# Two weight tiles on ScalarE's DMA queue, products of zeros at the start, and a last residual sum without GpSimd

## The chip, the cores and the metric

The kernel runs on one core of a Trainium2 chip. The metric is the device time of one execution in microseconds (us). A core has a matrix engine (TensorE, "PE" in the rows; its weight loads are "PEld"), VectorE ("DVE"), ScalarE ("ACT"), GpSimd ("POOL") and SyncE ("SP"). SP computes nothing here: it issues the transfers, which 16 DMA engines then carry out. Each engine takes its own instructions strictly in program order and waits on semaphores for the others.

## The reference

Two transformer blocks run one after the other on 256 tokens of width 1024, batch 1, in float32. The first block has two layers; each is

```
h = rmsnorm(x); proj = h @ w_in            # attention, indexer, HGRN and gate columns
x = x + (sigmoid(ga)*(attn @ w_proj_attn) + sigmoid(gb)*(hgrn @ w_proj_hgrn)) @ w_out
x = x + (silu(g) * u) @ w_ffn_out          # g, u = rmsnorm(x) @ w_ffn_in
```

The second block has one layer with a mixer of forgetting attention and a causal convolution, and a feed-forward network. Its last step is what the kernel ends with:

```
y = swiglu_ffn(h, w_ffn_in, w_ffn_out)
x = x + g2 * rms_norm(y, ffn_post_g)       # the result, 256 x 1024
```

## The kernel before

**Tiling.** Every weight matrix is cut into tiles of 128 x 1024 floats (512 KB), stored in the order of use in one array `W`. A tile is loaded into one of 4 `raw` buffers. ScalarE rounds it to `wH` and VectorE computes the rest `wL = raw - wH` (`do_split`); there are 6 buffers of each. TensorE multiplies with both in a reduced format and adds three products, wH·xH + wH·xL + wL·xH (`mm3`). A tile serves 24 products of 128 x 256 in the first layers. The input x, transposed, is the constant `xT`; it arrives in four pieces of 256 KB (`load_x(0)` to `load_x(3)`), each holding two of the eight chunks of the inner dimension. For every chunk ScalarE writes `xH` and VectorE `xL` (`scaled_split`), with a scale that comes from the array `params`. The first two weight tiles are loaded in halves (`CUT = 2`): the first half holds chunks 0 to 3, the second 4 to 7.

**Order.** The program is first recorded as a list of operations with their dependencies (`Recorder.record`). `Recorder.issue` then plays that list with estimated costs, picks on each engine the available operation of the highest urgency (the estimated length of the chain behind it plus `bias`), and emits the instructions of all engines in the order of the starts that it found. The plan has an engine "DMA" for the queue of SP, whose loads cost their bytes at 360 GB/s plus a latency, and starts at `FIRST_LOAD`. The chip then runs that fixed order, with its own durations. Table sets of ScalarE are loaded where the plan needs a function outside the current set (`load_tables`).

**The start.** SP issues params, the four pieces of x, the first half of weight tile 0, a piece of the constants, the second half of tile 0, a small weight matrix (`b<-in_small`), positions, and tiles 1 to 3. TensorE's first instruction is the first product of tile 0.

**The end.** `post(n, acc, last)` takes the four accumulators of the last product (token half t, column half h), and for each t computes 1/rms on VectorE from two squares that ScalarE sums (`inv_rms`, with the chain of short [128,1] operations in `rsqrt`), multiplies the accumulators with the weight row (`u`), and adds u·r to the residual in `xt` (an `E` buffer). For t = 1 the last step is one fused VectorE instruction for each h. In the last call t = 0 is done otherwise: ScalarE scales u by r and GpSimd adds it to `xt`. Each quarter is then sent out by a DMA of SP.

In the rows every recorded operation has line L408, the line that emits it, so they are told apart by tile names: `c` is any constant (xT, params, the matrix of ones), `t` any temporary of 512 columns, `side` and `mm` are accumulators, `small` the short columns.

Of the kernel before, what the change touches and what calls it, by code (L numbers as in the profile page):

```python
# [19 lines left out]
AF = mybir.ActivationFunctionType  # L20
# [3 lines left out]
D, T, NCH = 1024, 256, 8  # L24
GROUPS = 4
ON_V = (0, 4)
LAST = 0.0
FF, NJ = 2816, 11
LINE = 128

# [2 lines left out]
PLACE, ROOM = 28, 64  # L33

SCRATCH = 8192
OUT_SHAPE = [256, 1024]
EPS = 1e-6
NEG = -1e30
# [275 lines left out]
SETS = ("exp_and_others", "natural_log_exp_and_others", "silu_and_others")  # L314
TABLES = {AF.Exp: {0, 1}, AF.Tanh: {0, 2}, AF.Ln: {1}, AF.Silu: {2}, AF.Sin: {2}}
FIRST_LOAD = 500.0
LOAD_LATENCY, GATE_BIAS, LATER = 2000.0, 30000.0, -1e6
PRM_BIAS = 5000.0
TABLE_BIAS = -2000.0
# [32 lines left out]
class Recorder:  # L352
    def __init__(self, nc):
        self.ops = []
        self.bias, self.feed = 0.0, None
        self.load_tables = nc.scalar.preload_act_table_set
        for name, real in (("PE", nc.tensor), ("V", nc.vector), ("S", nc.scalar), ("DMA", nc.sync), ("G", nc.gpsimd)):
            setattr(self, name, Engine(self, name, real))

    def record(self, engine, real, method, args, kw):  # L360
# [50 lines left out]
    @staticmethod  # L411
    def cost(engine, method, args, kw, views, outs):
        n = int(np.prod((outs or views)[0].shape[1:]))
        psum = any(v.buf.space == "PSUM" for v in views)
        if engine == "DMA":
            v = (outs or views)[0]
            return max(v.shape[0] * n * 4 / 360.0, 640.0)
        if engine == "PE":
            if method == "transpose":
                return 109.0  # L420
            m = int(np.prod(args[1].shape[1:]))
            if args[1].dtype == F32R:
                return max(n * 0.4265, 109.0)
            cost = max(n, m) * 1.667 + 3.0
            if args[1].shape[0] == 64:

                return cost / 2

            return (cost + 81.0) / 4 if m == 32 else (cost + 53.0) / 2 if m == 64 and n > 64 else cost
        if engine == "S":  # L430
            ptr = sum(isinstance(kw.get(k), View) for k in ("bias", "scale"))
            return (51 if psum else 94) + 0.833 * n + 93 * ptr + (93 if "accum_out" in kw else 0)
        if method in ("max",):
            n = int(np.prod(args[1].shape[1:]))
        fast = not psum and method in ("tensor_copy", "tensor_scalar")
        ptr = sum(isinstance(a, View) for a in args[2:{"tensor_scalar": 4, "scalar_tensor_tensor": 3}.get(method, 2)])
        return (68 if method != "memset" else 7) + n / (1.92 if fast else 0.96) + 61 * ptr

    def issue(self):
# [12 lines left out]
                ops[d].users.append((op, lat))  # L452
        for op in reversed(ops):
            tail = max([u.rank + lat for u, lat in op.users], default=0.0)
            op.rank = tail + op.cost + (LOAD_LATENCY if op.engine == "DMA" else 0.0)
            op.urgency = op.rank + op.bias
            if QUANT and op.engine == "PE":
                op.urgency = op.urgency // QUANT * QUANT

        names = ["PE", "V", "S", "DMA", "G"]  # L460
        free_at = dict.fromkeys(names, 0.0)
        free_at["DMA"] = FIRST_LOAD
        pending = {e: [] for e in names}
        avail = {e: [] for e in names}
        slots, waiting, first, line = {}, {}, {}, {}
# [23 lines left out]
        while len(order) < len(ops):  # L489
# [91 lines left out]
                busy, left = busy + inside * rate, cost - inside  # L581
            op.start, op.end = t, t + cost
            free_at[e] = op.end
            done = op.end + (LOAD_LATENCY if e == "DMA" else 0.0)
            order.append(op)
            for b in op.bufs:
                if b.space == "PSUM":
# [43 lines left out]
def program(tc, I, out, pw, cw, tap=None, stop=None):  # L631
# [11 lines left out]
    with es:  # L643
# [8 lines left out]
        def body():  # L652
# [13 lines left out]
            def bank(tag="mm"):  # L666
                return new(psum, [128, 512], F32, tag=tag, bufs=4)
# [29 lines left out]
            A = lambda o, i, f, **k: S.activation(o, i, f, **k)  # L697


            prm = new(const, [128, I["params"].shape[1]])  # L700
            R.bias = PRM_BIAS
            DMA.dma_start(prm, I["params"])
# [23 lines left out]
            def load(i):  # L726
                if i < NT and i not in raw:
                    raw[i] = new(wp, [128, 1024], F32, tag="raw", bufs=N_RAW)
                    for k, c in enumerate(cuts(i)):
                        R.bias = FIRST[k] if i == 0 else 0.0  # L730
                        DMA.dma_start(raw[i][:, c], I["W"][i][:, c])
                    R.bias = 0.0

            def do_split(i):
# [797 lines left out]
            def post(n, acc, last):  # L1532
                gp = G[n][3]
                for t in range(2):
                    R.bias = (LAST if last else EARLY) if t == int(last) else 0.0
                    r = inv_rms(lambda h: acc[2 * t + h])
                    for h in range(2):
                        s = slice(h * 512, h * 512 + 512)
                        u = t512()
                        tt(u, acc[2 * t + h], gp[:, s], OP.mult)  # L1540
                        if last and t == 0:
                            A(u, u, AF.Copy, scale=r)
                            R.G.tensor_tensor(xt[:, t, s], xt[:, t, s], u, OP.add)
                        else:
                            stt(xt[:, t, s], u, r, xt[:, t, s], OP.mult, OP.add)
                        if last:
                            DMA.dma_start(out[t * 128:t * 128 + 128, s], xt[:, t, s])
                R.bias = 0.0
# [193 lines left out]
```

## Time and profile before

| | |
|---|---|
| time, three runs | 1110.72 us median (1109.97 to 1111.0) |
| the profiled execution | 1110.12 us, of which the span on the page is 1108.0 us |
| TensorE matmul busy | 1073.6 us, 97% of the span |
| VectorE busy | 855.5 us, 77% |
| ScalarE busy | 589.8 us, 53% |
| GpSimd busy | 7.4 us, 1% |
| moved by DMA | 217.47 MB, mean 196 GB/s |

TensorE is busy nearly all the time. What it is not busy adds up to 34.4 us (1108.0 - 1073.6), and most of that lies at the two ends: the first 9.57 us and the last 9 us. A change at the ends is therefore read from the time lines of the first 20 us and the last 10 us, and a share of busy time over the whole span says nothing about it.

### The profile page before, as it was taken

To read this page: it belongs to the slowest core of one execution; us is meant where nothing else is said; L and a number is where in the kernel's file an instruction comes from. 1 tells how busy PE (TensorE), PEld (TensorE's weight loads), DVE (VectorE), ACT (ScalarE), POOL (GpSimd) and SP (SyncE) were. 2 spreads that over 40 slices of the span, in tenths; PEclk is the share of its full clock that TensorE was granted. 3 is DMA by queue.
4 is the path that set the end of the run, shared out by engine and by line. 5 is a ranking of instruction groups with operands and counts; after the bars stand their busy time and mean duration, and the time that the engine had idled before them with its cause. 6 is when DMAs were issued, how large, how long until landed. Compare 5 with 4: busy or idle time off the path is not lost.

```text
span 1108.0 us, 22974 instructions
## 1 busy us (share of the span) xinstructions
PE 1073.6 (97%) x9388; PEld 1010.8 (91%) x9388; DVE 855.5 (77%) x1590; ACT 589.8 (53%) x902; POOL 7.4 (1%) x16
## 2 busy tenths in 40 slices
PE   6999999999999999999999999999899979999996
PEld 6988999999999999889999999999798568999995
DVE  7999968798966589999778999756799677454554
ACT  5745585544544467446846444444645665444442
POOL 1000000000000000000000000000000000000000
PEclk9999999999999999999999999999999999999999
DMA  7544536689966543645366889666377126556550
GB/s 262 177 156 156 166 125 191 221 302 335 348 221 212 196 149 131 210 135 172 118 197 223 293 329 370 212 196 197 116 217 199 63 77 200 178 184 218 189 173 38
DMA packets 59992, 217.47 MB, mean 196 GB/s; under 512 B 6872, under 2 KB 10096, under 8 KB 56816
## 3 DMA queue, kind: packets, MB, share of 16 engines
q1 hardware_dynamic: 59888, 216.02, 58.5%
q8 instruction: 73, 1.20, 0.4%
q14 instruction: 31, 0.25, 0.1%
HBM read 214.19 MB, written 1.63 MB: 195 GB/s over the span
## 4 chain that ended last, share of the span: by engine, by line
PE 85%; DVE 7%; ACT 3%; DMA 3%; issue 1%; SPq 0%; DVEq 0%; ACTq 0%
PE mm L408 59%; PE side L408 26%; DMA raw<-in_W 3%; DVE wL L408 3%; ACT t L408 1%; DVE t L408 1%; ACT wH L408 1%; DVE small L408 1%; DVE sc L408 1%; DVE c L408 1%; DVE b L408 1%; DVE xL L408 0%; ACT b L408 0%; ACT L615 0%; ACT c L408 0%
## 5 line engine op out<-in xcount | busy, mean ns | idle before, releaser
L408 ACT ACTIVATE wH<-raw 128x1024 fp32r<-128x1024 f32 (+1 forms) x390 | 369.3, 970 | 385.3 <-PE mm L408 217.1
L408 DVE TENSOR_TENSOR wL<-raw,wH 128x1024 fp32r<-128x1024 f32 (+1 forms) x390 | 424.6, 1111 | 137.1 <-ACT wH L408 136.0
L408 PE MATMUL mm<-xH,wH 128*128 128x256 f32 x1760 | 485.8, 279 | 9.6 <-ACT wH L408 9.6
L408 PE MATMUL mm<-xL,wH 128*128 128x256 f32 x1760 | 486.8, 278 | 0.5 <-DVE xL L408 0.5
L408 PE MATMUL mm<-xH,wL 128*128 128x256 f32 x1760 | 485.0, 278 | 0.8 <-DVE wL L408 0.8
L408 PEld LDWEIGHTS mm<-xH,wH 128*128 128x128 f32 x1760 | 330.0, 188 | 13.6 <-ACT wH L408 9.6
L408 PEld LDWEIGHTS mm<-xL,wH 128*128 128x128 f32 x1760 | 330.8, 188 | 4.9 <-issue 2.8
L408 PEld LDWEIGHTS mm<-xH,wL 128*128 128x128 f32 x1760 | 330.4, 188 | 3.1 <-DVE wL L408 1.7
L408 PE MATMUL side<-t,wH 128*128 128x256 f32 x704 | 122.5, 275 | 0.0
L408 PEld LDWEIGHTS side<-t,wH 128*128 128x128 f32 x704 | 106.5, 188 | 0.0
L408 PE MATMUL side<-t,wL 128*128 128x256 f32 x352 | 96.8, 275 | 0.0
L408 ACT ACTIVATE t<-t 128x512 f32<-128x512 f32 (+2 forms) x80 | 48.9, 619 | 41.3 <-DVE t L408 40.6
L408 PEld LDWEIGHTS side<-t,wL 128*128 128x128 f32 x352 | 66.1, 188 | 0.0
L408 DVE SCALAR_TENSOR_TENSOR E<-E,b 128x1024 f32<-128x1024 f32 x48 | 58.0, 1220 | 7.4 <-DMA E<-in_ada 7.4
L408 PE MATMUL side<-wH,t 128*128 128x512 f32 x176 | 56.6, 391 | 0.0
L408 DVE TENSOR_TENSOR t<-t,t 128x512 f32<-128x512 f32 (+2 forms) x78 | 53.1, 680 | 3.8 <-ACT t L408 2.9
L408 PE MATMUL mm<-b,wH 128*128 128x256 f32 x256 | 44.3, 275 | 0.0
L408 PE MATMUL side<-E,wH 128*128 128x256 f32 x256 | 44.1, 276 | 0.0
L408 PE MATMUL mm<-wH,xH 128*128 128x512 f32 x96 | 38.7, 410 | 3.1 <-ACT xH L408 2.7
L408 DVE TENSOR_TENSOR t<-mm,rstd 128x512 f32<-128x512 f32 (+1 forms) x50 | 33.7, 677 | 10.1 <-PE mm L408 9.7
L408 PE MATMUL mm<-wL,xH 128*128 128x512 f32 x96 | 39.1, 407 | 1.0 <-DVE wL L408 1.0
L408 PE MATMUL mm<-wH,xL 128*128 128x512 f32 x96 | 39.1, 409 | 0.0
(205 smaller groups left out, 1161.8 us busy)
## 6 DMA issues: line engine op xcount, KB each, us to landing
raw<-in_W SPq DMA_DIRECT2D x348, 512.0 KB, 4.4
E<-in_ada SPq DMA_DIRECT2D x24, 1024.0 KB, 7.3
b<-c SPq DMA_DIRECT2D x16, 128.0 KB, 5.6
c<-in_xT SPq DMA_DIRECT2D x4, 256.0 KB, 4.7
raw<-in_W SPq DMA_DIRECT2D x4, 256.0 KB, 5.4
b<-in_c SPq DMA_DIRECT2D x2, 512.0 KB
out_y<-E SPq DMA_DIRECT2D x4, 256.0 KB, 2.0
c<-E SPq DMA_DIRECT2D x4, 143.0 KB, 5.6
```

The costliest lines, as they stand in the source:

```text
L408: op.emit = lambda: getattr(real, method)(*[get(a) for a in args], **{k: get(a) for k, a in kw.items()})
```

## The change

There are three edits. The loads of weight tiles 0 and 1 (four halves) are issued by ScalarE and not by SP; for the plan this is a further engine "Q" beside "DMA". VectorE clears a tile of 128 x 128 floats, and TensorE multiplies it with itself 18 times, with a bias that puts these products ahead of all others. And in the last `post`, the half t = 0 ends like t = 1, with the fused VectorE instruction; the bias of the two halves changes with it.

```diff
-LAST = 0.0
+WARM = 18
+LOADERS = "DMA", "Q"
+ON_Q = 2
...
-        for name, real in (("PE", nc.tensor), ("V", nc.vector), ("S", nc.scalar), ("DMA", nc.sync), ("G", nc.gpsimd)):
+        for name, real in (("PE", nc.tensor), ("V", nc.vector), ("S", nc.scalar), ("DMA", nc.sync), ("Q", nc.scalar), ("G", nc.gpsimd)):
...
-        names = ["PE", "V", "S", "DMA", "G"]
+        names = ["PE", "V", "S", "DMA", "Q", "G"]
         free_at = dict.fromkeys(names, 0.0)
-        free_at["DMA"] = FIRST_LOAD
+        free_at["DMA"] = free_at["Q"] = FIRST_LOAD
...
+            zero = new(const, [128, 128])
+            V.memset(zero, 0.0)
+            warm = bank("side")
+            R.bias = 1e6
+            for _ in range(WARM):
+                PE.matmul(warm[:, :128], zero, zero, start=True, stop=True, skip_group_check=True)
+            R.bias = 0.0
...
-                        DMA.dma_start(raw[i][:, c], I["W"][i][:, c])
+                        (R.Q if i < ON_Q else DMA).dma_start(raw[i][:, c], I["W"][i][:, c])
...
             def post(n, acc, last):
...
-                    R.bias = (LAST if last else EARLY) if t == int(last) else 0.0
+                    R.bias = EARLY if t == 0 else 0.0
...
-                        if last and t == 0:
-                            A(u, u, AF.Copy, scale=r)
-                            R.G.tensor_tensor(xt[:, t, s], xt[:, t, s], u, OP.add)
-                        else:
-                            stt(xt[:, t, s], u, r, xt[:, t, s], OP.mult, OP.add)
+                        stt(xt[:, t, s], u, r, xt[:, t, s], OP.mult, OP.add)
```

Since the plan is made anew, instructions move beyond these lines. With buffer numbers left out, the order of the changed kernel differs from the old one in the first 1490 of some 8700 rows of TensorE, in the first 392 of some 1500 of VectorE, and in the first 191 of some 830 of ScalarE; then it is the same until the last `post`.

SP at the start. `c_87` (before) and `c_94` (now) are x, `in_params` the scales, `raw_106`/`raw_129` tiles 0 and 1 before. Before:

```order
L408 DMA c_83<-in_params 128x331
L408 DMA c_87<-in_xT 128x512 x4
L408 DMA raw_106<-in_W 128x512
L408 DMA c_108<-in_consts 128x194
L408 DMA raw_106<-in_W 128x512
L408 DMA b_81_118<-in_small 128x544
L408 DMA t_42_124<-in_pos 128x256
L408 DMA raw_129<-in_W 128x512
```

Now (`raw_105`, `raw_128` and `raw_152` are tiles 2, 3 and 4):

```order
L412 DMA c_85<-in_params 128x331
L412 DMA c_94<-in_xT 128x512 x2
L412 DMA raw_105<-in_W 128x1024
L412 DMA raw_128<-in_W 128x1024
L412 DMA c_94<-in_xT 128x512 x2
L412 DMA raw_152<-in_W 128x1024
L412 DMA c_172<-in_consts 128x194
L412 DMA b_83_177<-in_small 128x544
```

The halves of tiles 0 and 1 are gone from SP. The tiles 2 and 3 of 512 KB each now stand ahead of the last two pieces of x, and the small matrix stands behind tile 4.

ScalarE at the start, before:

```order
L615 ACT_TABLE_LOAD
L408 ACTIVATE c_100<-c_100 128x4
L408 ACTIVATE xH_110<-c_87,c_83 128x256 x5
L408 ACTIVATE wH_126<-raw_106 128x512
L408 ACTIVATE xH_110<-c_87,c_83 128x256 x2
L408 ACTIVATE wH_126<-raw_106 128x512
```

Now (`raw_87` is tile 0, `raw_101` tile 1, `t_29` to `t_32` are squares of x):

```order
L412 DMA raw_87<-in_W 128x512 x2
L412 DMA raw_101<-in_W 128x512 x2
L412 ACT_TABLE_LOAD
L412 ACTIVATE wH_112<-raw_87 128x512
L619 ACT_TABLE_LOAD
L412 ACTIVATE c_118<-c_118 128x4
L412 ACTIVATE wH_112<-raw_87 128x512
L412 ACTIVATE xH_140<-c_94,c_85 128x256 x4
L412 ACTIVATE t_29_158<-c_94 128x512
L412 ACTIVATE t_30_165<-c_94 128x512
L412 ACTIVATE xH_140<-c_94,c_85 128x256 x4
L412 ACTIVATE t_31_189<-c_94 128x512
```

Four issues lead, the rounding of tile 0 stands ahead of x, and there is a second table load in the stretch. The last two squares (`t_31`, `t_32`) and all of x stand ahead of the rounding of tile 1.

VectorE at the end, from the product with the weight row for the accumulator t = 1, h = 1 (`t_2120` before, `t_2122` now) back to 1/rms of t = 1. Before:

```order
L408 TENSOR_TENSOR t_2120_13579<-side_12059,b_1865_11740 128x512
L408 TENSOR_SCALAR small_13581<-small_13576 128x1
L408 SCALAR_TENSOR_TENSOR small_13585<-small_13576,small_13581 128x1
L408 TENSOR_TENSOR small_13587<-small_13585,small_13581 128x1
L408 SCALAR_TENSOR_TENSOR small_13589<-small_13587 128x1
```

Now:

```order
L412 SCALAR_TENSOR_TENSOR E_10347<-t_2111_13557,small_13577,E_10347 128x512
L412 TENSOR_SCALAR small_13600<-small_13597 128x1
L412 SCALAR_TENSOR_TENSOR E_10347<-t_2112_13569,small_13577,E_10347 128x512
L412 SCALAR_TENSOR_TENSOR small_13604<-small_13597,small_13600 128x1
L412 TENSOR_TENSOR t_2122_13606<-side_12080,b_1867_11761 128x512
L412 TENSOR_TENSOR small_13609<-small_13604,small_13600 128x1
L412 SCALAR_TENSOR_TENSOR small_13611<-small_13609 128x1
```

The two sums of t = 0 (`E_10347`) now stand between the first short operations of t = 1; the rows after them are the same in both.

## Rows read from the trace of the kernel before

**Rows 1.** The page: busy time of TensorE and VectorE, share of the span, instructions.

```profile
PE 1073.6 (97%) x9388; PEld 1010.8 (91%) x9388; DVE 855.5 (77%) x1590; ACT 589.8 (53%) x902; POOL 7.4 (1%) x16
```

**Rows 2.** Stretches: length, busy (instructions) by engine, granted clock, DMA share, GB/s.

```profile
2.00:16.00 14.00, 5.98 (x31) 5.57 (x32) 8.89 (x21) 9.64 (x20) 2.15 (x4) 1.00 0.96 323
16.00:39.00 23.00, 22.73 (x196) 22.32 (x195) 22.15 (x50) 16.47 (x22) 0.23 (x1) 1.00 0.56 186
160.00:1098.00 938.00, 924.78 (x7860) 876.18 (x7859) 708.12 (x1216) 488.97 (x728) 0.53 (x1) 0.99 0.60 200
```

**Rows 3.** Time line, start: start us, us, instruction, count [idle before <-releaser].

```profile
0.73 1.28 ACT L615 ACT_TABLE_LOAD   x1 [0.73 <-PEq L1734]
1.18 1.84 SPq L408 DMA_DIRECT2D c<-in_xT  x4
4.78 0.91 ACT L408 ACTIVATE xH<-c,c 128x256 fp32r<-128x256 f32 x2 [1.04 <-DMA c<-in_xT]
8.89 0.63 ACT L408 ACTIVATE wH<-raw 128x512 fp32r<-128x512 f32 x1 [0.78 <-DMA raw<-in_W]
9.57 0.58 PE L408 MATMUL mm<-xH,wH 128*128 128x256 f32 x1 [9.57 <-ACT wH L408]
12.19 1.14 ACT L408 ACTIVATE t<-c 128x512 f32<-128x512 f32 x2
```

**Rows 4.** Time line of TensorE, 13.2 to 16.5 us and 154 us.

```profile
13.24 0.41 PE L408 MATMUL mm<-xH,wH 128*128 128x256 f32 x1
13.45 0.39 PE L408 MATMUL mm<-xL,wH 128*128 128x256 f32 x1
16.42 0.38 PE L408 MATMUL mm<-xH,wL 128*128 128x256 f32 x1
154.37 0.38 PE L408 MATMUL side<-b,b 128*128 128x128 f32 x2
154.58 0.39 PE L408 MATMUL side<-b,AT 128*128 128x128 f32 x2
```

**Rows 5.** Time line of VectorE, 11.5 to 20.4 us.

```profile
11.56 0.29 DVE L408 CAST t<-t 128x256 f32<-128x256 int32 x1
12.93 1.48 DVE L408 TENSOR_TENSOR t<-t,t 128x512 f32<-128x512 f32 x2
14.44 0.42 DVE L408 TENSOR_TENSOR t<-t 128x256 f32<-128x256 f32 x1
14.78 0.72 DVE L408 TENSOR_TENSOR b<-b,b 128x544 fp32r<-128x544 f32 x1
15.68 4.70 DVE L408 TENSOR_TENSOR wL<-raw,wH 128x512 fp32r<-128x512 f32 x5
```

**Rows 6.** The time line of TensorE, those that waited between 39 and 90 us.

```profile
70.62 0.50 PE L408 MATMUL mm<-wL,xH 128*128 128x512 f32 x1 [0.84 <-DVE wL L408]
85.99 0.47 PE L408 MATMUL mm<-wH,xH 128*128 128x512 f32 x1 [0.41 <-DVE t L408]
```

**Rows 7.** A later wait of TensorE, and the stretch around it (columns of rows 2).

```profile
793.68 0.29 PE L408 MATMUL mm<-xH,b 128*8 128x256 f32 x1 [2.53 <-ACT xH L408]
790.00:800.00 10.00, 6.52 (x40) 4.47 (x39) 8.14 (x19) 6.91 (x14) 0.00 (x0) 0.83 0.27 100
```

**Rows 8.** Time line of VectorE and GpSimd, last 9 us.

```profile
1100.38 2.48 POOL L408 TENSOR_TENSOR E<-E,t 128x512 f32<-128x512 f32 x2 [894.55 <-DVE small L408]
1100.41 1.25 DVE L408 SCALAR_TENSOR_TENSOR small<-small,small 128x1 f32<-128x1 f32 x1
1101.69 1.19 DVE L408 TENSOR_TENSOR small<-small,small 128x1 f32<-128x1 f32 x1
1102.91 0.16 DVE L408 SCALAR_TENSOR_TENSOR small<-small 128x1 f32<-128x1 f32 x1
1103.37 0.16 DVE L408 TENSOR_TENSOR small<-small,small 128x1 f32<-128x1 f32 x1
1103.76 1.42 DVE L408 SCALAR_TENSOR_TENSOR E<-t,small,E 128x512 f32<-128x512 f32 x2
```

More of the change, by code (lines that the diff above doesn't have):

```diff
@@ L414, in cost @@
         psum = any(v.buf.space == "PSUM" for v in views)
-        if engine == "DMA":
+        if engine in LOADERS:
             v = (outs or views)[0]
@@ L454, in issue @@
             tail = max([u.rank + lat for u, lat in op.users], default=0.0)
-            op.rank = tail + op.cost + (LOAD_LATENCY if op.engine == "DMA" else 0.0)
+            op.rank = tail + op.cost + (LOAD_LATENCY if op.engine in LOADERS else 0.0)
             op.urgency = op.rank + op.bias
@@ L583, in issue @@
             free_at[e] = op.end
-            done = op.end + (LOAD_LATENCY if e == "DMA" else 0.0)
+            done = op.end + (LOAD_LATENCY if e in LOADERS else 0.0)
             order.append(op)
```

## The prediction, made before the change was run

> **What bounds the kernel now.** The page comes first: TensorE is busy 1073.6 of 1108.0 us and VectorE 855.5 [rows 1]. The stretches tell where that matters. From 160 to 1098 us TensorE is busy for 924.78 of 938 us, and the changed kernel has the same order there; a lead or a lag at 160 us is carried to the last product. Only the first 160 us and the end can change the time. From 16 to 39 us TensorE works 22.73 us of 23 with 196 products (0.116 us each), and VectorE 22.15: two engines are full side by side [rows 2]. Later TensorE waits for VectorE at 70.62 (0.84 us) and at 85.99 (0.41) [rows 6], so a VectorE that is late at 20 us has little room to recover in. At the start nothing can be multiplied until 9.57 us, when the first half of weight tile 0 has landed and been rounded (8.89) [rows 3]. Products then start 0.21 us apart (13.24, 13.45) [rows 4], against 0.116 later: the lower of TensorE's two clocks (1.2 and 2.4 GHz). The granted-clock column reads 1.00 there [rows 2], so the spacing is the evidence. At the end VectorE alone sets the time, with short dependent operations and two sums [rows 8].
>
> **The last sum.** Removed: two ScalarE scalings and two GpSimd additions (together 2.48 us). Added: two fused VectorE operations. While GpSimd adds, from 1100.38 to 1102.86, two short VectorE operations with two inputs last 1.25 and 1.19 us [rows 8]. From the first to the second is 1.28 us, from the second to the next 1.22. Undisturbed, two such steps take 0.39 (1103.37 to 1103.76). The neighbour's work costs 1.28 + 1.22 - 0.39 = 2.11 us on the path that sets the end. The two added operations stand on the same path; a pair of that kind takes 1.42 us, 1.35 without the overlap of its end with the next. Sum: 1.35 - 2.11 = -0.76 us. Between those short operations they also fill gaps of a few hundredths. Bounds: -0.5 (the added pair costs 1.6) to -1.0. The last pair and its two output transfers stay where they were; the first two transfers go earlier.
>
> **The queue.** Nothing in the trace shows a transfer issued by ScalarE. Its four issues cost between nothing and SP's price (four in 1.84 us [rows 3]); I take SP's. ScalarE starts at 0.73 us, so it is free at 2.6, and the table load (1.28 us [rows 3]) ends at 3.9. That hides behind the landing of tile 0's first half, which is issued at 0.7, half a microsecond before the x piece that landed for 4.78 [rows 3]. Call it 4.5. Rounding takes 0.63 us; the second table load 1.28, to 6.4; the second half is rounded by 7.2, x chunk 0 by 7.7, and VectorE's part of it, taken as long as ScalarE's (two in 0.91 us [rows 3]), makes the first product possible at 8.2, instead of 9.57. Chunks 1 to 3 follow at 0.45 us each, so TensorE has chunks 0 to 3 done at about 10.
>
> Then it must stop, because the last two pieces of x now stand behind tiles 2 and 3 on SP. By the shapes in the order, ahead of and including the last piece are params (128 x 331 x 4 bytes = 0.17 MB), x (1.05), tiles 0 and 1 (1.05) and tiles 2 and 3 (1.05): 3.3 MB. The 16 engines moved 323 GB/s from 2 us on, already 0.96 busy [rows 2]: 3.3 / 0.323 = 10.3 us, so 12.3 us; at a share of 1.00 (336 GB/s) 11.9. Landings come later than that count where more is queued behind: tile 0's first half ended the first 1.48 MB before, which makes 2 + 4.6 = 6.6 us by the same count, and it was used at 8.89 [rows 3], 2.3 us later. The bounds are 11.9 and 14.6. I take 13.0, nearer the low end, because two queues should fill the start of the transfers better; the piece before it is then there at 12.2.
>
> A rule speaks against this edit. The Trainium skill (DMA: Bandwidth & Descriptors, Issuing engines are not separate DMA queues) says that transfers of SP and ScalarE run on the same 16 engines and interleave, and that a second issuer saves only issue time. By it, no byte comes faster, which is the count above; with a queue of its own for each, the rival A below would hold. The share of 0.96 [rows 2] agrees with the rule, but no run here shows two issuers.
>
> From 13.0 us: chunks 6 and 7 are rounded by 13.9 and finished on VectorE at 14.4. ScalarE then makes the last two squares (two in 1.14 us [rows 3], to 15.0) ahead of the rounding of tile 1; VectorE adds them (two in 1.48 [rows 5]) to 15.9 and only then starts on tile 1's rest. Before, it started there at 15.68, and had by then also done a cast, the last addition of squares, the small weights and a scaling: 0.36 us, and 14.44 to 15.68 = 1.24 [rows 5]. **VectorE is 0.2 + 1.6 = 1.8 us behind.** TensorE: the third product of tile 1 starts after tile 1's first half, at 16.55; ten more products fit (to 17.7), then it waits for the second half, which stands behind tile 2: 15.9 + 0.65 + 1.13 + 0.65 = 18.3 (five such operations in 4.70 us, two of them halves [rows 5]). At 18.3 it has done 36 products. Before, 29 were done at 16.42 [rows 4] and (18.3 - 16.42) / 0.116 = 16 more by 18.3: 9 products or 1.05 us, and four short products of the norm (some 0.4 us) are still to come. **TensorE is 1.5 us behind.** The earlier first product gains nothing, since the wait in the middle takes it back. I take +1.5 for the head. For x at 11.9 the same steps give +0.4, for 14.6 +3.1.
>
> **The 18 products of zeros.** VectorE clears the tile right at its start; I let the products begin at 1.4 us. A product of two float32 tiles of this size takes 0.22 us at the higher clock (154.37 to 154.58 [rows 4]), 0.44 at the lower. All 18 last 4.0 to 7.9 us from 1.4: to 5.4 at best, 9.3 at worst. Before, the lower clock lasted from 9.57 to about 13.5, 4 us; so nine at either clock, to 7.4. The cover is the wait for x chunk 0 until 8.2; at the worst end it is gone and the first product comes 1.1 us later, still hidden by the wait at 10. What they buy is a higher clock at 8.2, when there are few products to do. Value: 0, between -0.2 and +0.3.
>
> **Sum.** Against the profiled execution (1110.12: span 1108.0 and 2.1 around it): -0.76 + 1.5 + 0 = 1110.9. It lies 0.6 us under the median of 1110.72, so 1111.5 for the median. A measurement tells about 0.2%, or 2.2 us, from no change; this is inside.
>
> **Rivals.**
> A, faster: two queues move their bytes independently. Then the last piece of x waits only for SP's own 2.3 MB, 2 + 7.0 = 9.0 us, 4 us before my 13.0. VectorE would be about 2.2 us ahead and TensorE is no longer held: 1110.7 - 0.8 - 2.2 = 1107.7. Against it is the share of 0.96; for it, that the start of the transfers was not full. Chance 0.15.
> B, faster by less: x lands by 11.9, and the new order of the first 100 us closes the waits at 70 and 86 us (1.25 us together [rows 6]): 1110.7 - 0.8 + 0.4 - 1.25 = 1109.1, to 1108 if a lag of VectorE is absorbed by its idle time. Chance 0.22.
> C, slower: the clock falls again in the gap. At 793.68 TensorE had waited 2.53 us, and in the 10 us around that the mean granted clock is 0.83 [rows 7]: (1 - 0.83) x 2 x 10 = 3.4 us at the lower level. My forecast has a gap of 2.7 us (10 to 12.7) and thin work on both sides. If the lower level holds for 3.4 us from 15.6, up to 1.7 us of products are lost, of which the wait for tile 1's second half hides 0.6: 1111.5 + 1.1 = 1112.6, and 1113.5 with x at 14. It decides if the clock is low after tile 1 is there. The zeros would have been for nothing. Chance 0.25.
> The Trainium skill (TensorE: Matmul & The Clock Gate, HAM oscillation) describes the same fall behind transfers that TensorE waits for, with half speed as the price. The row at 793 agrees; by that page alone C would be the likeliest.
> That the change does not do what it says: the products may end so late that the clock never counts; this is within the forecast.
>
> **How the numbers follow.** The forecast, x at 12.4 to 13.6 with no loss by the clock, has 0.38 and gives 1110.8 to 1112.2. Faster by over 0.2% (below 1108.5): A (0.15) and 0.10 of B. Slower (above 1112.9): 0.18 of C and 0.10 from the late end of the forecast. The rest, 0.47, is within 0.2%. The range leaves out the end of A and of C with late x: 1107.9 to 1113.6.
>
> **What would show it.** Right: the last x parts on ScalarE start after 12.5 us; TensorE has a gap of over 2 us between chunk 3 and chunk 4; the rest of tile 1 starts on VectorE no earlier than 15.5; at the end no short VectorE operation is over 0.3 us, and from the last product to the end it takes 0.8 us less. Wrong: x complete at 10 us or before; a table load or the issues on ScalarE of several us; a first product after 9.5; or a different lag at 160 us than at 20, which would mean that the middle of the new order decides, and not the start.

## The result, and the profile after

The changed kernel takes 1116.57 us (median of 6 runs, 1114.87 to 1117.48), the kernel before 1110.75 beside it: a ratio of 1.0056, 95% interval 1.0046 to 1.0066, so 5.1 to 7.3 us slower. The forecast was 1111.5 and no difference. The profiled span is 1114.6 us instead of 1108.0. The places are in the stretches (columns as in [rows 2]):

```profile
2.00:16.00 14.00, 11.04 (x61) 9.93 (x60) 7.63 (x17) 10.92 (x20) 2.17 (x4) 0.84 0.89 328
16.00:39.00 23.00, 22.85 (x189) 22.85 (x190) 21.36 (x49) 15.39 (x20) 0.00 (x0) 0.95 0.49 163
39.00:90.00 51.00, 48.38 (x361) 43.23 (x360) 46.60 (x106) 27.72 (x34) 0.00 (x0) 0.97 0.61 195
90.00:160.00 70.00, 66.73 (x892) 58.60 (x891) 64.56 (x180) 42.86 (x89) 0.53 (x1) 1.00 0.45 143
160.00:1098.00 938.00, 925.37 (x7891) 877.50 (x7891) 707.24 (x1215) 488.84 (x732) 0.53 (x1) 0.99 0.61 201
```

From 160 us on TensorE is as full as before (925.37 against 924.78 [rows 2]). From 39 to 160 us it is not. The two stretches of the kernel before, for comparison:

```profile
39.00:90.00 51.00, 49.58 (x362) 43.02 (x363) 48.17 (x115) 25.25 (x31) 0.00 (x0) 1.00 0.57 188
90.00:160.00 70.00, 69.82 (x942) 63.44 (x941) 61.15 (x173) 46.04 (x100) 0.52 (x1) 1.00 0.44 142
```

TensorE's waits in the changed kernel, in its time line (the bracket is the idle time ahead and what ended it). They answer to [rows 6], whose waits at 70 and 86 us are gone:

```profile
12.31 0.58 PE L412 MATMUL mm<-xH,wH 128*128 128x256 f32 x1 [2.14 <-ACT xH L412]
47.42 0.91 PE L412 MATMUL side<-t,c 128*32 128x128 f32 x16 [1.38 <-ACT t L412]
49.51 0.58 PE L412 MATMUL mm<-xH,wH 128*128 128x256 f32 x1 [1.18 <-DVE t L412]
147.20 1.24 PE L412 MATMUL side<-t,b 128*64 128x256 f32 x8 [0.45 <-ACT t L412]
149.65 1.15 PE L412 MATMUL side<-b,b 128*64 128x64 f32 x16 [0.35 <-ACT b L412]
152.37 1.16 PE L412 MATMUL side<-b,b 128*128 128x128 f32 x8 [1.57 <-DVE b L412]
163.44 0.33 PE L412 MATMUL side<-c,b 128*128 128x128 f32 x1 [0.32 <-ACT b L412]
```

The last product starts at 1105.96 us instead of 1098.35, 7.61 us later. This is the account of it, from the two traces:

- **Head, 1.6 us.** At 18.45 us TensorE has done 36 products, 4.14 us of work at 0.115 us each: 14.3 us lost. Before, 3.7 us of work were done at 16.42: 12.7 lost.
- **First place (46 to 53 us), 2.5 us.** Two waits of 1.38 and 1.18 us, and behind them the granted clock falls to 0.50 for 3.4 us, from 49.2 to 52.6; TensorE works from 49.51, so it loses 1.6 us of work. Against that stand four waits of before between 39 and 90 us, 1.67 us in all, that are not there now.
- **Second place (140 to 165 us), 3.4 us of waits.** Seven waits, 3.36 us; five of them over 0.3 us, four of which stand above.

The three come to 7.5 us, but they count waits only, and the near match with 7.61 is in part chance. A stricter measure is the lag at equal work: how much later the changed kernel is at moments up to which both traces have done the same set of TensorE's instructions, the zeros left out. By the times of the kernel before, it is 1.6 us at 37 us, 1.2 at 44, 5.6 at 55 (behind the first place), 3.4 at 86 (where the old waits are saved), 3.0 at 138 and 8.2 at 164 (behind the second place). Then it is 7.9 at 200 us, between 7.1 and 9.0 further on, and 7.6 at the last product. So the first place, less the old waits that it saves, costs 1.8 us, and the second costs 5.1. The same 247 instructions stand between the two products of each kernel below, and take 25.28 us before and 30.40 now:

```profile
138.33 0.28 PE L408 MATMUL mm<-xH,wL 128*128 128x256 f32 x1
163.61 0.36 PE L408 MATMUL mm<-xH,wL 128*128 128x256 f32 x1
141.38 0.28 PE L412 MATMUL mm<-xH,wL 128*128 128x256 f32 x1
171.78 0.28 PE L412 MATMUL mm<-xH,wL 128*128 128x256 f32 x1
```

Some 1.5 us of that difference lie outside the waits, at small products above all: from start to start, 12 side<-c,t take 1.0 us more and 24 side<-b,b 0.7.

The tail gives 1.04 us back: the last pair of sums starts at 1110.33 instead of 1103.76 [rows 8], 6.57 us later. That is the 6.6 us of the span.

Head and tail in rows: ScalarE's issues and its first table load, the zeros, the first product; two products on either side of the gap; the late x, the rest of tile 1 on VectorE, the 37th product; and one of VectorE's last short operations, none of which lasts 1.2 us any more, with the last pair of sums:

```profile
0.73 1.86 ACTq L412 DMA_DIRECT2D raw<-in_W  x4
2.62 1.28 ACT L412 ACT_TABLE_LOAD   x1 [2.62 <-issue]
1.42 5.90 PE L412 MATMUL side<-c 128*128 128x128 f32 x36 [1.42 <-DVE c L412]
7.76 0.38 PE L412 MATMUL mm<-xH,wH 128*128 128x256 f32 x1 [0.45 <-ACT xH L412]
9.22 0.28 PE L412 MATMUL mm<-xH,wH 128*128 128x256 f32 x1
9.34 0.32 PE L412 MATMUL mm<-xL,wH 128*128 128x256 f32 x1
13.42 0.41 PE L412 MATMUL mm<-xH,wH 128*128 128x256 f32 x1
13.64 0.41 PE L412 MATMUL mm<-xL,wH 128*128 128x256 f32 x1
11.75 1.71 ACT L412 ACTIVATE xH<-c,c 128x256 fp32r<-128x256 f32 x4 [1.80 <-DMA c<-in_xT]
15.41 4.69 DVE L412 TENSOR_TENSOR wL<-raw,wH 128x512 fp32r<-128x512 f32 x5
18.45 0.30 PE L412 MATMUL mm<-xH,wH 128*128 128x256 f32 x1
1109.94 0.16 DVE L412 TENSOR_TENSOR small<-small,small 128x1 f32<-128x1 f32 x1
1110.33 1.42 DVE L412 SCALAR_TENSOR_TENSOR E<-t,small,E 128x512 f32<-128x512 f32 x2
```

### The profile page after: what moved, and what is told of

Its sections match the earlier page's. It is cut to its first block, busy times and chain, and to the rows that moved or that the text cites. A ratio compares the mean times of both kernels' runs of the same rounds, so it can differ in the third digit from the quotient of the medians.

```text
span 1114.6 us, 23033 instructions
## 1 busy us (share of the span) xinstructions
PE 1083.3 (97%) x9424; PEld 1019.3 (91%) x9424; DVE 856.2 (77%) x1593; ACT 589.1 (53%) x901; POOL 4.7 (0%) x14
## 4 chain that ended last, share of the span: by engine, by line
PE 84%; DVE 7%; ACT 5%; DMA 2%; issue 1%; DVEq 0%; SPq 0%; ACTq 0%
PE mm L412 59%; PE side L412 25%; DVE wL L412 2%; ACT t L412 2%; DVE t L412 2%; DMA raw<-in_W 1%; ACT wH L412 1%; DVE small L412 1%; ACT L619 1%; DMA c<-in_xT 1%; DVE b L412 1%; DVE c L412 1%; DVE sc L412 0%; ACT b L412 0%; DVE xL L412 0%
```

## The experiments

The theory after the result: the edits cost and give what they were forecast to, and the loss comes from the new order in which the planner puts the first 165 us. The rival: the second queue or the zeros cost it on the chip, in any order. All ratios are to the kernel before on the same chip; 0.001 is 1.1 us.

**1. The last sum alone.** In the kernel before:

```
- R.bias = (LAST if last else EARLY) if t == int(last) else 0.0
+ R.bias = EARLY if t == 0 else 0.0
...
- if last and t == 0:
-     A(u, u, AF.Copy, scale=r)
-     R.G.tensor_tensor(xt[:, t, s], xt[:, t, s], u, OP.add)
- else:
-     stt(xt[:, t, s], u, r, xt[:, t, s], OP.mult, OP.add)
+ stt(xt[:, t, s], u, r, xt[:, t, s], OP.mult, OP.add)
```

> The kernel before with one of the three edits: the last sum's first half as two fused operations on VectorE instead of ScalarE and GpSimd. Order and start are those of before. Theory (the change loses in the order of its first 165 us, and its tail gains): the two traces give the tail 1.04 us less (last product 7.61 us later, last pair of sums 6.57 us later), so 1.0 us under before: 1109.7, ratio 0.9991. Rival (the order of the tail gives nothing by itself, the pair of sums was merely met by other work): within 0.3 us of before.

Ratio 0.9986 (0.9977 to 0.9995), 0.6 to 2.6 us faster. The tail gains by itself; in the trace the last pair of sums starts 4.37 us behind the last product, 5.41 before, the same 1.04 us.

**2. All three edits, the order of before.** The planner takes the loads of tiles 0 and 1 as SyncE's, so every engine's order stays; the zeros are emitted ahead of the plan:

```
+ DMA.dma_start(raw[i][:, c], I["W"][i][:, c], **({"queue": nc.scalar} if i < ON_Q else {}))
...
+ for emit in self.ahead:                 # memset and 18 products
+     emit()
+ for op in sorted(order, key=lambda o: (not o.early, o.start, o.index)):
```

> All three edits on the chip (four loads on ScalarE's queue, 18 products of zeros, the last sum on VectorE), but every engine's instructions in the order of before: the loads are planned as SyncE's, and the zeros stand outside the plan. Theory (the new order of the middle costs 6 us: 2.6 at 46 to 53 us and 3.4 at 140 to 165): those two stretches are as in before, so the time is that of before plus at most the head's 1.6 us less the tail's 1.0: 1109 to 1111.5. Rival A (the second queue or the zeros cost the time on the chip, whatever the order): 1116 to 1117. Rival B (half of each): about 1113.

Ratio 1.0003 (0.9994 to 1.0012). Against run 1 on the same chip, queue and zeros together cost 0.0017 or 1.9 us; the two intervals just touch. TensorE is busy 50.10 and 69.72 us in the two stretches where the changed kernel has 48.38 and 66.73, and has no wait of 0.12 us or more between 39 and 60 us:

```profile
39.00:90.00 51.00, 50.10 (x376) 43.92 (x375) 48.97 (x117) 26.48 (x32) 0.00 (x0) 1.00 0.57 191
90.00:160.00 70.00, 69.72 (x940) 63.24 (x939) 61.40 (x169) 45.41 (x99) 0.53 (x1) 1.00 0.44 143
```

**3. The new order alone.** The changed kernel with the queue's engine put back to SyncE and the zeros planned but not emitted:

```
- ... ("Q", nc.scalar) ...
+ ... ("Q", nc.sync) ...
...
+ if unsent:
+     op.emit = lambda: None
```

> The order of the changed kernel on TensorE, VectorE and ScalarE and its last sum, but no products of zeros and no load from ScalarE: the four loads of tiles 0 and 1 go out on SyncE at the places of the plan, between the x pieces. Theory (the order decides): TensorE waits again 2 to 3 us at 46 to 53 us and 3 to 4 us at 140 to 165 us, time 1114 to 1118. Rival (the queue or the zeros decide): without them the new order runs as well as that of before, 1109 to 1111.

Ratio 1.0063 (1.0050 to 1.0075). With neither queue nor zeros, the whole loss is there, and so are the waits, one by one:

```profile
48.08 0.91 PE L413 MATMUL side<-t,c 128*32 128x128 f32 x16 [1.06 <-ACT t L413]
50.17 0.39 PE L413 MATMUL mm<-xH,wH 128*128 128x256 f32 x1 [1.18 <-DVE t L413]
146.56 1.25 PE L413 MATMUL side<-t,b 128*64 128x256 f32 x8 [0.46 <-ACT t L413]
151.72 1.16 PE L413 MATMUL side<-b,b 128*128 128x128 f32 x8 [1.57 <-DVE b L413]
```

Runs 2 and 3 settle it: the order costs the time, and the rival falls. The 247 instructions of the second place take 30.15 us here. The first place looks otherwise: the clock does not fall behind it, and the lag is 2.6 us at 37 and 2.7 at 86 us, so its waits are paid back by the old ones that are saved.

**4. A later start in the order of before.** One tile that nobody reads, loaded first on SyncE:

```
+ DMA.dma_start(idle, I["W"][9])          # ahead of the plan
```

> The kernel before with one more load of a whole weight tile (128x1024 floats, 0.52 MB, read by nobody) ahead of everything on SyncE's queue; all else in its order. At 323 GB/s it is 1.6 us of transfers. Theory (a lag of the head in an unchanged order is carried one for one to the end, as the prediction took it): 1.6 us over before, 1112.3, with the waits at 70 and 86 us still there and of their old size. Rival A (the waits later on take a lag up): 0 to 0.8 us. Rival B (lateness of the weights alone opens new waits in the middle, in any order): 3 us or more, 1114 and up.

Ratio 1.0017 (1.0008 to 1.0026), 0.9 to 2.9 us. In its trace the first product is 0.78 us later (10.35) and VectorE's copy rstd 1.14 (28.99); the waits at 70 and 86 us are 0.84 and 0.79, no new one opens. So rival B is out. In this trace the lag is carried, 0.8 us at 37 and 1.2 at 164. In run 2, in the order of before too, it shrinks from 1.95 us at 37 to 0.65 at 164. Whether a lag goes through one for one, the interval does not tell.

**5 and 11. The zeros, in either order.** The changed kernel without them (planned, not emitted), and the kernel before with the last sum and the zeros, all loads on SyncE:

> The changed kernel without the 18 products of zeros and their memset; order, queues and last sum are its own. Against the run of its order alone (the loads on SyncE, no zeros) it tells what the second queue is worth in that order; against the changed kernel, what the zeros are worth. In the trace of the changed kernel the granted clock stood at 0.50 from about 12 to 18 us and from 49.5 to 52.5 us; in the run of the order alone it did not. Theory (the order costs, the zeros and the queue give or take under 1.5 us each): 1114.5 to 1117. Rival A (the zeros bring on the two falls of the clock, 1.6 and 1.65 us): 1113. Rival B (the queue costs by itself): 1118 and up.

> The kernel before in its own order with the last sum on VectorE and the 18 products of zeros ahead of the plan; all loads on SyncE. It differs from the run with all three edits in the order of before only in the queue, and from the run of the last sum alone only in the zeros. Theory (zeros are worth nothing or little, since the first products wait for data; the queue costs about 1.5 us in this order, where TensorE waited 2.47 us at 10.31 and 1.57 us at 15.75): 1108 to 1109.5, near the last sum alone (0.9986 of before). Rival A (the zeros give the first 20 products the full clock, 0.1 us each, and that is kept): 1106.5 to 1107.5. Rival B (the zeros cost, and the queue costs nothing): 1110 and up.

Ratios 1.0045 (1.0033 to 1.0057) and 0.9994 (0.9985 to 1.0002). Without the zeros the changed kernel comes out 1.2 us faster, with them the last sum loses 0.9 of its gain; each difference is within its intervals. Runs 2 and 11 differ in the queue only, 0.0009 of the ratio or 1.0 us, unresolved too. The zeros are worth nothing that could be measured here. In run 5's trace neither fall of the clock is there, but without the zeros its products are 0.21 us apart until 16.4 us, and 36 of them are done at 18.44 us, with the zeros at 18.45.

**6. One table load moved.** In the changed kernel ScalarE loads a table at 45.17 us, just ahead of the squares that TensorE waits for at 47.42. The sines go ahead of two weight tiles (pairs: operation, ahead of which):

```
+ MOVES = ((118, 444), (117, 471))
```

> The changed kernel with three instructions of ScalarE at other places and nothing else: the table load and the first sine (c<-t), which stand at 45.17 us between a weight tile and the squares t<-mm, go two weight tiles ahead, and the second sine goes ahead of the squares. The squares then wait for nothing but their weight tile, some 1.3 us earlier, and the sines are done some 4 us earlier. Theory (TensorE's waits of 1.38 us at 47.42 and 1.18 us at 49.51 come from this table load's place): both close to under 0.4 us and the fall of the clock behind them goes, so 2.2 to 4.2 us under the changed kernel: 1112.3 to 1114.3. Rival A (the weight tiles that are now 1.3 to 1.7 us later bring a wait of their own): 1115.5 to 1117. Rival B (TensorE waits there for the late weights in any case): no change, 1116.5.

Ratio 1.0064 (1.0051 to 1.0077): no gain. The waits are 1.70 and 1.72 us, because the weight tile behind the table load is late for VectorE:

```profile
44.23 1.23 DVE L413 TENSOR_TENSOR wL<-raw,wH 128x1024 fp32r<-128x1024 f32 x1 [1.15 <-ACT wH L413]
46.85 0.91 PE L413 MATMUL side<-t,c 128*32 128x128 f32 x16 [1.70 <-ACT t L413]
49.48 0.35 PE L413 MATMUL mm<-xH,wH 128*128 128x256 f32 x1 [1.72 <-DVE t L413]
```

The theory of the table load falls; rival A holds.

**7 and 8. The other table load moved, and both.** The logarithm that stands ahead of two evictions at 145.27 us goes to an idle stretch of ScalarE:

```
+ MOVES = ((49, 1647), (51, 1647), (50, 1647), (52, 1675))
```

> The changed kernel with four small instructions and one table load at other places and nothing else: the logarithm c<-c with its table load, which stands at 145.27 us on ScalarE ahead of the two evictions t<-side, goes to ScalarE's idle stretch of 3.52 us ahead of the weight tile of 139.58 us, and the three small operations on VectorE that feed it go 7.7 us ahead. What it computes is read first at 395 us of the plan. Theory (the chain from 142 to 157 us is late by this table load): t<-side starts 1.2 to 1.5 us earlier and TensorE's seven waits of 3.36 us shrink by 1.0 to 1.5: 1115.0 to 1115.5. Rival A (all of it hangs there): 3.3 us less, 1113.2. Rival B (the chain hangs on VectorE or on the exponentials, not on the table): no change, 1116.5.

> The changed kernel with both moves: the first sine's table load and the two sines ahead, and the logarithm with its table load ahead. Theory (the two places are apart, each a table load that stands ahead of what TensorE waits for): the gains add, 3.2 to 5.7 us under the changed kernel, 1111 to 1113.3. Rival (an earlier TensorE meets the next late operation): the gains overlap and less than the larger of the two alone is left, 1113 to 1115.

Ratios 1.0037 (1.0025 to 1.0050) and 1.0072 (1.0060 to 1.0084). Run 7 looks like a gain of 2.1 us, but its waits don't say so. The evictions do come earlier (3.16 us behind the exponentials instead of 4.61), and the first two waits close; the third grows from 1.57 to 2.29:

```profile
149.65 1.16 PE L413 MATMUL side<-b,b 128*128 128x128 f32 x8 [2.29 <-DVE b L413]
```

All waits of that place sum to 3.74 us, not 3.36. From the end of the first place's last wait to that of 163.44 us, the changed kernel takes 113.93 us, run 7 112.38 and run 3, with the logarithm unmoved, 112.35. The difference to the changed kernel is the fall of the clock behind 49.5 us, which neither run shows. So the table load is not the cause of the second place either: the same 247 instructions take 30.34 us. In these two traces run 7's gain is the clock; whether that holds for the medians is open, and with the same move in runs 10 and 14 it was 1.1 and 0.8 us, within the intervals.

**9, 10, 13 and 14. ScalarE's and VectorE's old order at the first place.** First regrouped by hand, without and with the logarithm's move; then 41 operations of VectorE and 17 of ScalarE put exactly into the order of before, without and with it:

```
+ queue = queues[e]                       # e: VectorE, ScalarE
+ queue[at:at + len(block)] = [by[k] for k in block]
```

> The changed kernel with ScalarE and VectorE in another order between 28 and 50 us, nothing else: both pairs of logarithms together and both tanh together, as before, so that one table load of three goes; the sines two weight tiles ahead; and on VectorE the operations that follow them (c, sr, cr and the eviction t<-mm that frees an accumulator) ahead of two to three weight tiles. Moving the sines alone made it no faster: TensorE's two waits were 1.70 and 1.72 us, with VectorE busy or waiting for weight tiles up to the same 48.5 us. Theory (the whole order of ScalarE and VectorE there decides, not the table's place alone): the two waits, 1.38 and 1.18 us in the changed kernel, fall under 0.6 us together and the clock stays up, 2 to 4 us under the changed kernel: 1112.3 to 1114.5. Rival (VectorE is behind from the start, whatever stands where): the waits keep over 2 us in all, 1116 to 1118.

> The same, and the logarithm with its table load ahead, which alone gave 2.1 us. Theory (two separate places): 4 to 6 us under the changed kernel, 1110.5 to 1112.5. Rival (the gain of the first place is taken up at the second): as with the logarithm alone, 1114.3.

> The changed kernel with 41 operations of VectorE (from the copy rstd to the last of the small t<-t of that stretch, about 30 to 53 us) and 17 of ScalarE (from the first |x| to the second sine) in the order in which the kernel before has the same operations, and nothing else: TensorE, SyncE, and all that comes after keep the changed kernel's order. In every run in the order of before the eviction's factor cr came 13.4 to 13.8 us after rstd on VectorE, in every run in the new order 17.7 to 18.0. Theory (VectorE's and ScalarE's order between 28 and 50 us is what TensorE waits for at 46 to 51 us): cr comes under 15 us after rstd, the two waits (1.38 and 1.18 us) fall under 0.6 us together without others of that size between 39 and 60 us, and the time is 1 to 4 us under the changed kernel: 1112.5 to 1115.5. Rival (TensorE's own new order wants other things at other times, so that half of the old order fits it worse): new waits of 2 us or more between 39 and 60 us, 1116.5 to 1120.

> The same with the logarithm and its table load ahead of the weight tile at 139 us, which alone gave 2.1 us. Theory (two separate places): 2 us under the run before this one, 1110.5 to 1113.5. Rival (as in the hand-made regrouping, where the logarithm's move gave 1.1 us of its 2.1): 1 us under it.

Ratios 1.0089 (1.0076 to 1.0102), 1.0079 (1.0066 to 1.0091), 1.0069 (1.0057 to 1.0081), 1.0062 (1.0050 to 1.0074): none better than the changed kernel. VectorE did what was wanted: cr, which stood 18.05 us behind rstd, stands 13.43 behind it in run 13, and the wait at 47 us shrinks to 0.33. But 3.57 us of waits are there, at other places, the last of them for a transfer:

```profile
41.22 0.34 PE L413 MATMUL side<-c,t 64*128 64x64 f32 x2 [1.61 <-DVE t L413]
48.26 0.43 PE L413 MATMUL side<-t,c 128*32 128x128 f32 x8 [0.33 <-ACT t L413]
55.36 1.13 PE L413 MATMUL side<-c,iq 64*128 64x256 f32 x6 [1.63 <-DMA c<-c]
```

**16, 17 and 18. All three engines' old order, at one place, the other, both.** The same with TensorE's operations in the blocks:

> The changed kernel with the operations that its plan starts between 24 and 60 us (289 of TensorE, 74 of VectorE, 29 of ScalarE) in the order in which the kernel before has the same operations, on all three engines; the rest, the loads and the zeros are its own. With ScalarE and VectorE alone in the old order TensorE waited 3.57 us there (at 41, 48 and 55 us) instead of 2.56. Theory (the three engines' orders belong together, and the new one of TensorE asks for results before VectorE can have them): with all three the waits between 39 and 60 us fall under 0.6 us, and the time is 2 to 3.6 us under the changed kernel: 1113 to 1114.5. Rival (VectorE, 2.6 us late at rstd, is late for any order): 2 us or more of waits stay, 1116 to 1118.

> The changed kernel with the operations that its plan starts between 115 and 170 us (467 of TensorE, 105 of VectorE, 69 of ScalarE) in the order of the kernel before, on all three engines; the rest is its own. In the trace of the changed kernel TensorE has no product to do between its 16 products side<-b,b that end at 150.8 us and the eight at 152.37 us that need VectorE's answer to them, where the kernel before has 22 products mm between the same two groups; and moving the logarithm left the waits of that stretch at 3.7 us, so that the table load was not what held it. Theory (TensorE's order there has nothing to fill a round trip with): the waits of 140 to 165 us, 3.36 us, fall under 0.6 us, and the time is 2.5 to 3.4 us under the changed kernel: 1113 to 1114. Rival (the accumulators or weight tiles that these products need are not there yet): the waits come back elsewhere between 115 and 250 us, no gain, 1116 to 1117.

> The changed kernel with both stretches in the order of the kernel before. Theory (the two places and the head are the whole loss): 4.5 to 7 us under the changed kernel, 1109.5 to 1112, as the run with all edits in the old order throughout (1.0003 of before). Rival (one stretch gives back what the other gains): 1113 to 1116.

**Run 17 is the proof for the second place**: 1.0034 (1.0023 to 1.0046), 2.4 us under the changed kernel's ratio (the intervals just touch). A single wait of 0.33 us (at 141.43) stands where seven were, TensorE is busy 69.67 of the 70 us, and the 247 instructions take 25.71 us instead of 30.40. Not all of these 4.7 us stay: a new wait of 0.72 us stands at 186.66, and the lag at equal work, 1.2 us at 164, is 3.0 at 282 and 2.65 at the last product.

```profile
90.00:160.00 70.00, 69.67 (x937) 63.00 (x936) 61.72 (x170) 44.85 (x98) 0.53 (x1) 1.00 0.42 138
186.66 0.51 PE L413 MATMUL side<-E,wH 128*128 128x256 f32 x2 [0.72 <-ACT wH L413]
```

What the new order lacks there is seen in the kernel before, and run 17 has it again. Between its 16 products of 64 columns and the eight that need VectorE's answer to them stand 22 products mm, 2.5 us of work; their first and last:

```profile
145.34 1.15 PE L408 MATMUL side<-b,b 128*64 128x64 f32 x16
146.41 0.38 PE L408 MATMUL mm<-xH,wH 128*128 128x256 f32 x1
148.82 0.28 PE L408 MATMUL mm<-xH,wL 128*128 128x256 f32 x1
148.94 1.05 PE L408 MATMUL side<-b,b 128*128 128x128 f32 x8
```

In the changed kernel the same two groups (149.65 and 152.37 above) follow each other with nothing between, and the round trip over VectorE is waited out. The products mm need accumulators, and VectorE empties four of those in one row only behind it. Run 17 put the order of all three engines back, so it does not tell whether TensorE's order or these late evictions hold the products:

```profile
151.56 0.75 DVE L412 TENSOR_TENSOR b<-b,t 128x256 f32<-128x256 f32 x2
154.75 2.48 DVE L412 TENSOR_TENSOR t<-mm,hr 128x512 f32<-128x512 f32 x4
```

**Run 16 went the other way**, 1.0107 (1.0093 to 1.0121), and run 18 with it, 1.0087 (1.0073 to 1.0101). The two waits of the first place are gone, but TensorE waits for 0.85 us at 41 and for 4.66 at 55 us; in run 18, where the second place is closed too, for 0.83 and 4.12. Run 16 in rows:

```profile
55.18 2.07 PE L413 MATMUL side<-c,iq 64*128 64x256 f32 x6 [4.66 <-DMA c<-c]
45.33 0.41 DVE L413 TENSOR_TENSOR c<-t,t 64x256 f32<-64x256 f32 x1
40.82 9.88 SPq L413 DMA_DIRECT2D raw<-in_W  x5
50.75 0.55 SPq L413 DMA_DIRECT2D c<-c  x1
```

The copy c<-c is ready at 45.74 and goes out at 50.75, because on SyncE it stands behind weight loads that wait for VectorE to free their buffers. SyncE kept the new order in that run: 18 tiles are loaded ahead of the copy, 15 in the order of before, where it was ready at 43.47 and went out at 43.49. By this wait the first place needs four queues in one order, SyncE's too; run 2, which has all four, has no wait there. A run with SyncE's part alone put back as well was not made, so for the first place it is not shown which part of the order opens its waits.

**12 and 15. Another order, by a number that does nothing on the chip.** In the kernel before, and with the last sum on VectorE:

```
- FIRST_LOAD = 500.0
+ FIRST_LOAD = 700.0
```

> The kernel before with one number of the plan changed: the first load may start at 700 ns of the plan's clock, not 500. On the chip no queue, load or operation is added or removed; the order of SyncE is word for word the same, but TensorE, VectorE and ScalarE come out in another order in some 50 places each from 30 us on. Theory (an order that the plan has not been tuned on opens waits of its own in the first 165 us): 1112 to 1116, ratio 1.001 to 1.005. Rival (the orders that the plan gives are about equally good, and only the changed kernel's is unlucky): within 1 us of before.

> The kernel before with the last sum on VectorE and the plan's first load at 700 ns, which alone gave 0.9986 and 0.9972 of before. Theory (the tail and the order of the first 165 us are apart, so the gains add): 0.9958, 1105.1 at a median of 1109.8. Rival (the order's gain lies in the tail too, where TensorE and VectorE also differ in a few places): 0.9972, 1106.7.

Ratios 0.9972 (0.9962 to 0.9983) and 0.9970 (0.9958 to 0.9982). My expectation of a loss was wrong in its sign: the order differs in some 50 places on TensorE and is 3.1 us better. Its waits at 69 and 85.67 us are 0.29 and 0.52, against 0.84 and 0.41 [rows 6], and from 39 to 90 us TensorE is busy 50.18 us instead of 49.58; that accounts for 0.6 us. The trace does not show the rest: at equal work run 12 is 1.6 us ahead at 200 us, level at 300 and 2.4 ahead at the end, and 2.1 of these come between 766 and 947 us, where run 4, in the order of before, gains 2.4 us against the same trace of before. The last sum adds nothing that shows on top. Both beat both kernels; 1106.43 us with 1109.42 beside it is the best time of the study.

## Why the prediction was wrong, step by step

- **The last sum: right.** Forecast -0.76, by the traces -1.04, by run 1 -0.6 to -2.6 us. The short operations last 0.15 to 0.23 us with GpSimd out of the way.
- **The queue: right in its steps, in part by luck in its sum.** First product 7.76 (forecast 8.2), chunks 0 to 3 done at 10.2 (10), a gap of 2.14 us (over 2), x rounded from 11.75 to 13.46 (to 13.9), tile 1's rest at 15.41 (15.9; no earlier than 15.5 was named as the mark), 36 products at 18.45 (18.3), a lag of 1.6 us (1.5). VectorE's copy rstd starts at 30.48 instead of 27.85, 2.6 us later; some 0.6 of that is a shuffle that now stands ahead of it, so VectorE is about 2 us behind (forecast 1.8).
- **Rival A is out.** The rate from 2 to 16 us is 328 GB/s with two issuers, 323 with one [rows 2]. The Trainium skill (DMA: Bandwidth & Descriptors, Issuing engines are not separate DMA queues) says that transfers of either issuer run on the same 16 engines; the trace agrees.
- **The zeros: right in time, and rival C's clock came.** They end at 7.32 (forecast 7.4), and the products behind are 0.12 us apart (9.22 to 9.34). In the gap the granted clock falls, stands at 0.50 from 12 to 18 us, and the products from 12.31 to 18.45 are 0.21 apart. This took the place of the wait for tile 1's second half that the forecast had there. VectorE has that half ready at 17.8 (the row at 15.41: two halves and a whole tile, 2.4 us), so the fall costs some 0.6 us more than the wait would have, and the steps ahead of it were some 0.5 us early. So C was not an addition of 1.1 us to the head, and 18.45 against 18.3 is luck: another road to the same time. The Trainium skill (TensorE: Matmul & The Clock Gate, HAM oscillation) describes a fall to half speed behind transfers that TensorE waits for; the stretch above agrees, behind a wait of 2.14 us.
- **The step that failed: "a lead or a lag at 160 us is carried to the last product".** Behind 160 us it holds within 1.1 us (8.2 us at 164, 7.6 at the end), but the sum used it from 18 us on and put the order between 20 and 160 us at nothing, without a reason. Only rival B looked there, and asked only what old waits it would close. Those closed, as B said (1.67 us in all). New ones of 5.9 us opened, with slower products and a fall of the clock beside them: the lag of 1.6 us grew to 8.2, of which the second place is 5.1. Nothing in the sum had room for them. The head's 1.6 and the tail's -1.0 alone would have given 1110.7 us in the profiled execution, next to the forecast of 1110.9; it took 1116.5.
- **What could have been seen.** The new order itself shows it without a time: on TensorE the two groups side<-b,b in a row where 22 products stood between, on SyncE the copy c<-c behind 18 tiles instead of 15. The prediction's last paragraph had named a different lag at 160 us than at 20 as the mark of this case (1.6 and 8 us came); it gave the case neither a chance nor a price, and the range ended at 1113.6.

My own explanation after the result fell as well: that ScalarE's table loads at 45 and 145 us hold TensorE. Moved, they left the waits as large or made them larger, with VectorE and the missing products behind them (runs 6 to 8).

## What to carry to other kernels

When a planner makes a new order out of a small edit, the edit and the order are two changes: apply the edit with the old order held, and the new order without the edit, before explaining either. In a new order, look for groups on the full engine that need each other's answer over another engine, and count what stands between them; an instruction that seems to cause a wait can be only its last link, and moving that alone uncovers the next one. Put the orders of all queues back together, the one that issues transfers included. And measure a lag where both traces have done the same work: sums of waits came out at 3.4 us for a place that cost 5.1.

## What was not expected of the hardware

TensorE's clock behaved in two ways that the granted column alone would hide. In the kernel before it reads 1.00 from the start [rows 2], while products are 0.21 us apart until 13.67 us. With zeros ahead (run 11) they are 0.12 apart from 10.39 to 11.10, and then, with TensorE busy for 2.00 of 2 us, 0.21 apart from 11.23 to 13.8, where the column reads 0.50:

```profile
10.98 0.28 PE L414 MATMUL mm<-xH,wL 128*128 128x256 f32 x1
11.10 0.33 PE L414 MATMUL mm<-xH,wH 128*128 128x256 f32 x1
11.44 0.42 PE L414 MATMUL mm<-xH,wL 128*128 128x256 f32 x1
12.00:14.00 2.00, 2.00 (x11) 1.91 (x9) 1.90 (x4) 2.00 (x5) 0.00 (x0) 0.50 1.04 375
```

So the zeros did not remove the slow stretch; they moved it behind the first products. Behind the first place the clock fell in some traces only: in the changed kernel and in runs 6 and 8, not in runs 3, 5, 7 and 17. The two waits ahead of it sum to 2.56, 3.42 and 3.40 us in the first three, and to 2.17 to 2.32 us in the other four. In these four the lag at 86 us is within 0.15 us of that at 37 us, in the first three 1.8 to 2.7 us more: in the traces the first place costs time only where the waits are long and the clock falls. No run varied these waits alone, so what decides is open.
